# A two-layer hybrid decoder step: compressed attention rows as one block, sample rows of the scan at once, norms in pairs

## The chip, the cores and the metric

The kernel runs on one core of a Trainium2 chip. The metric is the device time of one execution in microseconds (us), the median over runs.

## The reference

One inference step of two layers over 512 prompt positions and 8 sample positions (one new token for each of 8 sequences with a past of 1024), model width 1024, all in float32. Layer 0 is a mixer, in which a Mamba-2 scan (32 heads in four groups) and sparse attention (16 heads in two key groups) share one input and one output projection. Layer 1 is a Conformer convolution with a layer norm inside. Behind each layer stands a feed-forward block with a width-3 convolution. Every one of the four parts is wrapped in two norms:

```python
def rms_norm(x, g):
    y = x * lax.rsqrt(jnp.mean(x * x, axis=-1, keepdims=True) + EPS)
    return y * g
...
hp = hp + rms_norm(mix, g[1])      # after the mixer or Conformer
...
hp = hp + rms_norm(f, g[3])        # after the feed-forward block
```

An attention output is the gated sum of three parts. The first is over compressed rows (31 for the prompt, each from 32 positions), the others over selected blocks and over a window of 512:

```python
s_c = jnp.einsum('btghd,bngd->btghn', qg, kc)
p_c = masked_softmax(s_c, m_c)
o_c = jnp.einsum('btghn,bngd->btghd', p_c, vc)
...
o = g[..., 0:1] * o_c + g[..., 1:2] * o_s + g[..., 2:3] * o_w
```

The scan's recurrence is `h = exp(dt a) h + dt B x`, `y = C h`, then `y + d_skip x`, times `silu(z)`. The prompt does it in four chunks of 128; a sample position takes a single step from its stored state.

## The kernel before, in words

**Layout.** Activations lie with channels on partitions: eight blocks of 128 channels (`KD`), 520 columns (512 prompt, 8 sample). Columns are worked in two halves, `HALF`, of 256 and 264. A float32 product is done as three products of a type with fewer bits (`split` makes a high part on ACT and a low part on DVE; `mm3` and `dense`, lines 312 to 314).

**Order of work.** A scheduler orders each engine's instructions by their dependences and the program's order; tiles are taken from pools with a number of buffers, and a pool's space is used again after release. Loads go mostly through SP's DMA queue, some through POOL's and ACT's.

**Attention** (`attention`, line 1102) runs 16 steps: four groups of four heads (`hg`) by four blocks of 128 queries (`b`). A step makes the scores of four heads with 32 compressed rows (`pc`) and with the window and selected rows (`Ps`), takes the softmax, and multiplies by the gates. `turned` (line 1182) transposes the weights of four heads into `pT` on PE, and splits them into `pth` (ACT) and `ptl` (DVE); two products with the values `VB` add up in `po`. The compressed part is the last of these turns, 32 rows by 512 columns, with `VC`. Tiles of the input projection for the scan (`xz_tile`) run between the steps; the last steps have none.

**Scan** (`scan_group`, line 1302) runs four groups `g` of four channel blocks `t`. Each loads `xs` and `cum` (the running decay of 512 positions, then 8 decays and 8 step sizes of the samples), makes decay products `dc`, states `hst` and `y`. The sample rows of a block are seven DVE operations at lines 1387 to 1395. POOL adds `yt` to `y` (line 1382) and splits the gated output of the group before (`x0ls`, `x1ls`), while PE does the output projection (`out_block`).

**Norms.** `postnorm` (line 377) takes a half of a part's result (`facc`), squares the eight blocks on ACT, adds squares on DVE in groups (`sumsq`, line 322), sums over partitions by a product with `ones`, takes Ln and Exp on ACT (`rstd`), and adds the normed blocks to `h` by two DVE operations each (lines 385 and 387). `prenorm` (line 358) gives the next part's input: scaled and split blocks of `h`, and the sum of their squares, whose root is put in later. `boundary` (line 520) chains them between two parts, named a to d. In ACT's code, functions stand in tables; `ACT_TABLE_LOAD` is the change of a table.

## Time and profile before

| what | value |
|---|---|
| median of 3 runs | 1960.81 us (1960.59 to 1962.98) |
| profiled execution, its own time | 1961.67 us |
| its span | 1959.9 us |
| PE busy | 1835.2 us, 94% |
| DVE busy | 1415.3 us, 72% |
| ACT busy | 974.4 us, 50% |
| POOL busy | 189.5 us, 10% |
| mean granted clock of PE | 0.97 |

The span is the time from the first to the last instruction that the profile shows. A busy PE is one with a product under way; products overlap, so that what a product costs is seen from its start to the next start. Idle time is shown with the work that ended it. Engines wait in the order of their own queues: a waiting instruction holds all behind it.

### The profile page before, as it was taken

To read this page: it belongs to the slowest core of one execution; us is meant where nothing else is said; L and a number is where in the kernel's file an instruction comes from. 1 tells how busy PE (TensorE), PEld (TensorE's weight loads), DVE (VectorE), ACT (ScalarE), POOL (GpSimd) and SP (SyncE) were. 2 spreads that over 40 slices of the span, in tenths; PEclk is the share of its full clock that TensorE was granted. 3 is DMA by queue.
4 is the path that set the end of the run, shared out by engine and by line. 5 is a ranking of instruction groups with operands and counts; after the bars stand their busy time and mean duration, and the time that the engine had idled before them with its cause. 6 is when DMAs were issued, how large, how long until landed. Compare 5 with 4: busy or idle time off the path is not lost.

```text
span 1959.9 us, 38005 instructions
## 1 busy us (share of the span) xinstructions
PE 1835.2 (94%) x14449; PEld 1706.1 (87%) x14449; DVE 1415.3 (72%) x3385; ACT 974.4 (50%) x2093; POOL 189.5 (10%) x226
## 2 busy tenths in 40 slices
PE   6998889999998799998999999999989899999997
PEld 5997888988887588987999999998667789999997
DVE  5764768888887698968667766574786865666766
ACT  3223446676666577646555433355127755444433
POOL 0000021101000003130000211001111000000000
PEclk9999998999998799989999999999999999999999
DMA  8446254444321274543245433222433223444421
GB/s 296 114 140 197 76 190 130 149 138 129 126 90 57 92 243 136 157 143 100 87 143 165 132 105 109 87 81 53 119 107 119 87 87 116 122 119 120 148 62 49
DMA packets 125947, 240.90 MB, mean 123 GB/s; under 512 B 16499, under 2 KB 63236, under 8 KB 125444
## 3 DMA queue, kind: packets, MB, share of 16 engines
q1 hardware_dynamic: 120676, 221.45, 36.9%
q0 software_dynamic: 4000, 13.73, 2.2%
q10 hardware_dynamic: 1088, 3.29, 0.5%
q8 instruction: 114, 1.87, 0.4%
q14 instruction: 69, 0.57, 0.1%
HBM read 200.75 MB, written 30.88 MB: 118 GB/s over the span
## 4 chain that ended last, share of the span: by engine, by line
PE 43%; DVE 5%; ACT 3%; DMA 2%; issue 1%; SPq 0%; POOL 0%; DVEq 0%; ACTq 0%; POOLq 0%
PE up L312 8%; PE up L313 8%; PE up L314 8%; PE dn L312 4%; PE dn L313 4%; PE dn L314 4%; PE dn L624 2%; PE pw L312 1%; PE pw L313 1%; PE pw L314 1%; PE ns L333 1%; DMA raw_dn<-in_w_down 1%; DVE xf L385 1%; DVE h L387 1%; DVE facc L631 1%
## 5 line engine op out<-in xcount | busy, mean ns | idle before, releaser
L312 PE MATMUL dn<-gh,wh_dn 128*128 128x256 f32 (+1 forms) x704 | 198.0, 285 | 4.8 <-ACT gh L463 2.6
L314 PE MATMUL dn<-gh,wl_dn 128*128 128x256 f32 (+1 forms) x704 | 198.9, 284 | 0.0
L313 PE MATMUL dn<-gl,wh_dn 128*128 128x256 f32 (+1 forms) x704 | 198.4, 283 | 0.0
L451 DVE SCALAR_TENSOR_TENSOR c<-up,vec,c 128x511 f32<-128x511 f32 (+2 forms) x216 | 138.9, 645 | 16.1 <-ACT c L448 15.7
L312 PEld LDWEIGHTS dn<-gh,wh_dn 128*128 128x128 f32 x704 | 131.5, 189 | 6.8 <-DVE facc L478 3.7
L313 PEld LDWEIGHTS dn<-gl,wh_dn 128*128 128x128 f32 x704 | 133.1, 189 | 0.1
L314 PEld LDWEIGHTS dn<-gh,wl_dn 128*128 128x128 f32 x704 | 132.8, 189 | 0.0
L464 POOL TENSOR_TENSOR gl<-gm,gh 128x520 fp32r<-128x520 f32 (+2 forms) x54 | 61.8, 1145 | 700.6 <-ACT gh L463 700.5
L446 DVE TENSOR_TENSOR up<-up,rsx 128x520 f32<-128x520 f32 (+2 forms) x108 | 65.0, 603 | 81.5 <-PE up L314 79.9
L478 DVE TENSOR_TENSOR facc<-dn,facc 128x256 f32<-128x256 f32 (+1 forms) x160 | 66.2, 423 | 66.4 <-PE dn L314 66.1
L293 ACT ACTIVATE wh_up<-raw_up 128x1024 fp32r<-128x1024 f32 x68 | 72.0, 1058 | 71.8 <-PE up L313 46.5
L312 PE MATMUL acc<-x0hm,wh_xz 128*128 128x256 f32 x320 | 96.3, 301 | 6.9 <-ACT u L1001 4.5
L294 DVE TENSOR_TENSOR wl_up<-raw_up,wh_up 128x1024 fp32r<-128x1024 f32 x68 | 83.1, 1222 | 23.0 <-ACT wh_up L293 22.9
L314 PE MATMUL acc<-x0hm,wl_xz 128*128 128x256 f32 x320 | 94.3, 295 | 0.0
L313 PE MATMUL acc<-x0lm,wh_xz 128*128 128x256 f32 x320 | 94.1, 294 | 0.0
L313 PE MATMUL acc<-x1lm,wh_xz 128*128 128x264 f32 x320 | 92.8, 290 | 0.0
L312 PE MATMUL acc<-x1hm,wh_xz 128*128 128x264 f32 x320 | 92.6, 289 | 0.0
L448 ACT ACTIVATE c<-up,vec 128x520 f32<-128x520 f32 (+2 forms) x108 | 74.9, 695 | 34.8 <-DVE up L446 34.4
L314 PE MATMUL acc<-x1hm,wl_xz 128*128 128x264 f32 x320 | 92.1, 288 | 0.0
L293 ACT ACTIVATE wh_dn<-raw_dn 128x1024 fp32r<-128x1024 f32 (+1 forms) x48 | 47.4, 988 | 87.7 <-PE dn L313 62.8
L294 DVE TENSOR_TENSOR ptl<-pT,pth 128x512 fp32r<-128x512 f32 (+1 forms) x96 | 65.0, 684 | 25.8 <-ACT pth L293 25.6
L293 ACT ACTIVATE pth<-pT 128x512 fp32r<-128x512 f32 (+1 forms) x96 | 56.3, 595 | 53.1 <-PE pT L1186 49.9
(584 smaller groups left out, 6859.7 us busy)
## 6 DMA issues: line engine op xcount, KB each, us to landing
raw_up<-in_w_up SPq DMA_DIRECT2D x68, 512.0 KB, 3.8
raw_xz<-in_w_in SPq DMA_DIRECT2D x40, 512.0 KB, 4.8
raw_dn<-in_w_down SPq DMA_DIRECT2D x32, 512.0 KB, 3.7
raw_wo<-in_w_out SPq DMA_DIRECT2D x24, 512.0 KB, 4.2
raw_pw<-in_w_pw SPq DMA_DIRECT2D x24, 512.0 KB, 3.8
spill<-uth SPq DMA_DIRECT2D x40, 260.0 KB, 2.0
st<-in_st SPq DMA_DIRECT2D x40, 256.0 KB, 4.2
cc<-in_c_cmp SPq DMA_DIRECT2D x64, 128.0 KB, 2.6
```

What stands on the lines that cost most here:

```text
L293: nc.scalar.activation(hi, src, AF.Copy)
L294: (eng or nc.vector).tensor_sub(lo, src, hi.bitcast(F32))
L312: nc.tensor.matmul(ps, hi[:, wc], xh, start=first, stop=False)
L313: nc.tensor.matmul(ps, hi[:, wc], xl, start=False, stop=False)
L314: nc.tensor.matmul(ps, lo[:, wc], xh, start=False, stop=last)
L333: nc.tensor.matmul(ps, ones, acc[:, :n], start=i < group, stop=i == len(ks) - 1)
L446: nc.vector.tensor_mul(u(a, e0), u(a, e0), rv[:, a:e0])
L448: nc.scalar.activation(c[:, rs], u(r0, r1), AF.Identity, bias=V("fb", l * 44 + mt), scale=W(2, mt))
L451: nc.vector.scalar_tensor_tensor(c[:, a:e], u(a - d, e - d), W(2 - d, mt), c[:, a:e], op0=ALU.mult, op1=ALU.add)
L464: nc.gpsimd.tensor_sub(gl[:, rs], gm[:, rs], gh[:, rs].bitcast(F32))
L478: nc.vector.tensor_add(f, ps, f)
L624: nc.tensor.matmul(ps[i * 32:i * 32 + 32], cw[m][:, 4 * q + i], x4[m][:, i, cs], start=q == 0, stop=q == NQ[m] - 1)
```

## The change

Three parts. **Compressed rows:** the weights of four heads over 32 compressed rows are transposed as one 128x128 block; `VC` holds, for each head, a block of 128 rows that is zero outside that head's 32 rows; eight products of 128x128 go into the four quarters of `po`, ahead of the other parts. The compressed values of a group are computed in four copies of rows (`vc`), and `VC` is split from them when the key group changes. The query rows are loaded a block at a time. **Sample rows:** two DMAs gather decays and step sizes of all 16 blocks into `cumS`; POOL copies the sample columns of `x` into `smp`; `sample_rows` does three operations for all blocks at the scan's start, `sample_group` four operations for each group. **Norms:** squares, sums of squares, the product with the norm and the addition to `h` are done for two blocks at once; the norm's gain is put in by ACT, in place, and the sums come in groups half as long, in pairs.

```diff
-SQE = 2
+SQE = 1
...
-SQP = 4
-SQR = 8
-SQL = (1, 4)
+SQP = 2
+SQR = 4
+SQL = (1, 2)
...
+    def sumsq2(ps, src, group):
+
+        n = ps.shape[-1]
+        for i in range(KD // 2):
+            sq = P["bq"].tile([128, 2, 266], F32, tag="sq", name="sq", bufs=3)[:, :, :n]
+            last = nc.scalar.activation(sq, src(2 * i), AF.Square)
+            if i % group:
+                nc.vector.tensor_add(acc, acc, sq)
+            else:
+                acc = sq
+            if i % group == group - 1 or i == KD // 2 - 1:
+                for j in range(2):
+                    nc.tensor.matmul(ps, ones, acc[:, j], start=i < group and j == 0, stop=i == KD // 2 - 1 and j == 1)
         return last
...
     def postnorm(wk, psp, hf, f, l, i, group=SQP, done=lambda k: None):
         c0, c1 = HALF[hf]
         ps = psp(c1 - c0)
-        last = sumsq(wk, ps, lambda k: f[:, k], range(KD), group)
+        last = sumsq2(ps, lambda k: f[:, k:k + 2], group)
+        for k in range(KD):
+            nc.scalar.activation(f[:, k], f[:, k], AF.Copy, scale=V("ng", (l * 4 + i) * 8 + k))
         r = rstd(wk, ps, 1.0 / D, "rs2", last if hf == 0 else None)
         done_["post%d" % hf] = done_["exp"]
-        for k in range(KD):
-            t = wk.tile([128, 266], F32, tag="xf", name="xf", bufs=XFB)
-            nc.vector.scalar_tensor_tensor(t[:, :c1 - c0], f[:, k], V("ng", (l * 4 + i) * 8 + k), r,
-                                           op0=ALU.mult, op1=ALU.mult)
-            nc.vector.tensor_add(h[:, k, c0:c1], h[:, k, c0:c1], t[:, :c1 - c0])
-            done(k)
+        for k in range(0, KD, 2):
+            f2, h2 = f[:, k:k + 2], h[:, k:k + 2, c0:c1]
+            nc.vector.tensor_mul(f2, f2, r[:, None].to_broadcast([128, 2, c1 - c0]))
+            nc.vector.tensor_add(h2, h2, f2)
+            done(k + 1)
...
+                VC = tp.tile([128, 4, 2, 64], F32R, tag="VC", name="VC", bufs=1)
+                nc.gpsimd.memset(VC.bitcast(F32), 0.0)
+                for hh in range(4):
+                    rw = slice(32 * hh, 32 * hh + 32)
+                    split(VC[rw, hh, 0], VC[rw, hh, 1], vc[rw, g])
             for b in range(4):
...
+                qh = tp.tile([128, 2, 128], F32, tag="qh", name="qh", bufs=2)
+                nc.sync.dma_start(qh, d_q[hg][:, :, b * 128:b * 128 + 128])
...
-                parts.append((VC[:, g], [pc[:, hh] for hh in range(4)], 32))
-                for k, (v, ps4, kn) in enumerate(parts):
-                    ph, pl = turned(ps4, kn)
...
+                pT = gen(128, "pT")
+                nc.tensor.transpose(pT, pc.rearrange("p h k -> p (h k)"), ident)
+                ph, pl = parted(pT)
+                for hh in range(4):
+                    for p in (ph, pl):
+                        nc.tensor.matmul(po[:, hh * 128:hh * 128 + 128], VC[:, hh].rearrange("p a d -> p (a d)"), p,
+                                         start=hh == 0 and p is ph, stop=False)
...
+        cd = tp.tile([128, 16, 2 * NB], F32, name="cumS")
+        for r in range(2):
+            nc.gpsimd.dma_start(cd[r * 64:r * 64 + 64], d_rows[r::2, S:528].rearrange("(o m) t -> o m t", o=1)
+                                .to_broadcast([64, 16, 2 * NB]))
+        xsk = tp.tile([128, 16, NB], F32, name="xskS")
+
+        def sample_rows():
+
+            nc.scalar.activation(smp[:, :, 1], cd[:, :, 0:NB], AF.Exp)
+            nc.vector.tensor_mul(xsk, smp[:, :, 0], VV("dsk")[:, :, None].to_broadcast([128, 16, NB]))
+            nc.vector.tensor_mul(smp[:, :, 0], smp[:, :, 0], cd[:, :, NB:])
+
+        def sample_group(g, y, bcs):
+
+            gs = slice(4 * g, 4 * g + 4)
+            ys = tp.tile([128, 4, NB], F32, tag="ys", name="ys", bufs=2)
+            nc.vector.tensor_mul(hC[:, gs], hC[:, gs], smp[:, gs, 1])
+            nc.vector.tensor_mul(ys, smp[:, gs, 0], bcs[:, 1][:, None, :].to_broadcast([128, 4, NB]))
+            nc.vector.tensor_add(hC[:, gs], hC[:, gs], xsk[:, gs])
+            nc.vector.tensor_add(y[:, :, S:T], hC[:, gs], ys)
...
-                dtx, es = smp[:, 4 * g + t, 0], E[:, S:T]
-                nc.vector.tensor_copy(smp[:, 4 * g + t, 1], es)
-                ys = tp.tile([128, 2, NB], F32, tag="ys", name="ys", bufs=2)
-                for r in range(2):
-                    sl = slice(r * 64, r * 64 + 64)
-                    nc.vector.tensor_mul(dtx[sl], xs[sl, S:T], cum[sl, r, T:528])
-                nc.vector.tensor_mul(ys[:, 0], hC[:, 4 * g + t], es)
-                nc.vector.tensor_mul(ys[:, 1], dtx, bcs[:, 1])
-                nc.vector.tensor_add(ys[:, 0], ys[:, 0], ys[:, 1])
-                nc.vector.scalar_tensor_tensor(y[:, t, S:T], xs[:, S:T], V("dsk", 4 * g + t), ys[:, 0],
-                                               op0=ALU.mult, op1=ALU.add)
+                if t == 0:
+                    sample_group(g, y, bcs)
```

Beside this, the squares and input copies of the mixer's first norm take their buffers from a pool of their own, `cum` and `E` lose their sample columns, and the stored states of the last group are read one group earlier.

The order of instructions moves at three places. First POOL at the end of the scan: `y<-y,yt` is the addition of line 1382, the others split the gated output for the output projection. Before:

```order
L294 TENSOR_TENSOR x0ls<-y,x0hs 128x256 x4
L294 TENSOR_TENSOR x1ls<-y,x1hs 128x264 x4
L1382 TENSOR_TENSOR y<-y,yt 128x384 x7
L294 TENSOR_TENSOR x0ls<-y,x0hs 128x256 x4
L294 TENSOR_TENSOR x1ls<-y,x1hs 128x264 x4
L1382 TENSOR_TENSOR y<-y,yt 128x384
L294 TENSOR_TENSOR x0ls<-y,x0hs 128x256 x4
L294 TENSOR_TENSOR x1ls<-y,x1hs 128x264 x4
```

After:

```order
L294 TENSOR_TENSOR x1ls<-y,x1hs 128x264 x4
L1442 TENSOR_TENSOR y<-y,yt 128x384 x8
L294 TENSOR_TENSOR x0ls<-y,x0hs 128x256 x4
L294 TENSOR_TENSOR x1ls<-y,x1hs 128x264 x4
L294 TENSOR_TENSOR x0ls<-y,x0hs 128x256 x4
L294 TENSOR_TENSOR x1ls<-y,x1hs 128x264 x4
```

The last addition stood behind eight splits of the group before, and now stands ahead of them.

Second DVE at the start of the scan, group 0, block 0 (`xde` is the input times step size and decay, `dc` the decay products, `hst` the states). Before:

```order
L1344 TENSOR_TENSOR xde<-xT,te 128x512
L1311 COPY bcs<-bcs 128x8
L1387 COPY smp<-E 128x8
L1392 TENSOR_TENSOR ys<-hC,E 128x8
L1393 TENSOR_TENSOR ys<-smp,bcs 128x8
L1394 TENSOR_TENSOR ys<-ys 128x8
L1395 SCALAR_TENSOR_TENSOR y<-xs,vec,ys 128x8
L1368 TENSOR_TENSOR dc<-dc,cbm 128x512
L1356 SCALAR_TENSOR_TENSOR hst<-hst,dec,states 128x64 x2
```

After:

```order
L1404 TENSOR_TENSOR xde<-xT,te 128x512
L1369 COPY bcs<-bcs 128x8
L1349 TENSOR_TENSOR smp<-smp,cumS 128x16x8
L1356 TENSOR_TENSOR ys<-smp,bcs 128x32
L1428 TENSOR_TENSOR dc<-dc,cbm 128x512
L1416 SCALAR_TENSOR_TENSOR hst<-hst,dec,states 128x64 x2
```

The operation that reads the gathered `cumS` stands ahead of the decay products and the states; ACT's exponential of `cumS` likewise stands ahead of `x0hn`, the split of attention's output.

Third ACT at boundary b, behind the first feed-forward block (`lnv` is the Ln and `rs` the Exp of a norm, `ge` the GELU of the feed-forward block, `wh_pw` the split of Conformer weights). Before:

```order
L459 ACTIVATE ge<-c_16270 128x264
L327 ACTIVATE sq<-facc 128x256
L339 ACT_TABLE_LOAD
L293 ACTIVATE wh_pw_16615<-raw_pw_16613 128x1024
L448 ACTIVATE c_16302<-up,vec 128x264
L348 ACTIVATE lnv<-ns,epsT 128x256
L349 ACTIVATE rs_16101<-lnv 128x256
```

After:

```order
L341 ACTIVATE sq<-facc 128x2x256
L354 ACT_TABLE_LOAD
L471 ACTIVATE fstg<-up 128x10
L476 ACT_TABLE_LOAD
L476 ACTIVATE ge<-c_16195 128x264
L398 ACTIVATE facc<-facc,vec 128x256 x2
L293 ACTIVATE wh_pw_16516<-raw_pw_16514 128x1024
L465 ACTIVATE c_16227<-up,vec 128x264
L363 ACT_TABLE_LOAD
L363 ACTIVATE lnv<-ns,epsT 128x256
L364 ACT_TABLE_LOAD
L364 ACTIVATE rs_16053<-lnv 128x256
```

The load for the norm now stands ahead of the last GELU, so that a load back follows at once, and Ln and Exp have one each. In the whole program there are 33 table loads, where there were 27.

## Rows read from the trace of the kernel before

**Rows 1.** The page, first part: busy time of each engine, share, instructions.
```profile
PE 1835.2 (94%) x14449; PEld 1706.1 (87%) x14449; DVE 1415.3 (72%) x3385; ACT 974.4 (50%) x2093; POOL 189.5 (10%) x226
```

**Rows 2.** Busy by stretch (PE, PEld, DVE, ACT, POOL), clock, DMA share, GB/s.
```profile
300.00:606.00 306.00, 297.06 (x2309) 268.63 (x2307) 260.61 (x823) 199.78 (x500) 26.35 (x39) 0.98 0.40 123
606.00:668.00 62.00, 51.30 (x219) 34.59 (x216) 44.95 (x129) 34.31 (x84) 0.00 (x0) 0.78 0.07 22
690.00:850.00 160.00, 153.81 (x1300) 143.46 (x1297) 147.99 (x432) 111.12 (x280) 35.38 (x37) 0.99 0.54 166
910.00:960.00 50.00, 39.72 (x278) 36.95 (x278) 38.97 (x88) 33.02 (x66) 5.80 (x7) 0.90 0.15 46
```

**Rows 3.** Timeline of PE, 606 to 625 us: start, length, engine, line, operation.
```profile
607.10 0.28 PE L1124 MATMUL sc<-KL,QS 128*128 128x256 f32 x1
607.22 0.28 PE L1123 MATMUL sc<-KH,QS 128*128 128x256 f32 x1
...
607.83 0.39 PE L1199 MATMUL po<-pth,VB 128*128 128x512 f32 x1
608.05 0.60 PE L1186 MATMUL pT<-cst,pt 128*128 128x128 f32 x4
```

**Rows 4.** Timeline of PE, 338 to 342 us, inside attention.
```profile
339.29 0.49 PE L1199 MATMUL po<-pth,VC 32*128 32x512 f32 x1
339.71 0.38 PE L312 MATMUL acc<-x0hm,wh_xz 128*128 128x256 f32 x1
```

**Rows 5.** Timeline of all engines, 663.5 to 668.5 us, last attention step.
```profile
664.41 0.59 ACT L293 ACTIVATE pth<-pT 32x512 fp32r<-32x512 f32 x1 [0.73 <-DVE ptl L294]
...
665.03 0.68 DVE L294 TENSOR_TENSOR ptl<-pT,pth 32x512 fp32r<-32x512 f32 x1 [0.62 <-ACT pth L293]
```

**Rows 6.** Timeline, 668 to 690 us, start of the scan; idle time in brackets.
```profile
670.84 0.16 DVE L1387 COPY smp<-E 128x8 f32<-128x8 f32 x1
...
670.91 0.16 DVE L1392 TENSOR_TENSOR ys<-hC,E 128x8 f32<-128x8 f32 x1
...
681.20 0.34 DVE L1391 TENSOR_TENSOR smp<-xs,cum 64x8 f32<-64x8 f32 x2 [2.61 <-DMA cum<-d_rows]
```

**Rows 7.** Timeline, 846 to 854 us, end of the scan.
```profile
847.93 0.75 DVE L1378 SCALAR_TENSOR_TENSOR y<-xs,vec,yd 128x512 f32<-128x512 f32 x1 [0.59 <-PE yd L1372]
...
850.95 0.99 POOL L1382 TENSOR_TENSOR y<-y,yt 128x384 f32<-128x384 f32 x1
...
851.96 0.70 DVE L1397 TENSOR_TENSOR y<-y,zt 128x520 f32<-128x520 f32 x1 [2.92 <-POOL y L1382]
```

**Rows 8.** Groups by line and form, whole span: DVE, ACT and PE.
```profile
L651 DVE TENSOR_TENSOR facc<-facc,nmu 128x528 f32<-128x528 f32 x4 | 2.6, 704 | 2.5 <-ACT nmu L649 2.5
...
L366 ACT ACTIVATE x0ha<-h,vec 128x256 fp32r<-128x256 f32 x8 | 4.0, 498 | 0.4 <-DVE h L387 0.4
...
L333 PE MATMUL ns<-sq,ones 128*128 128x264 f32 x56 | 17.2, 414 | 5.9 <-DVE sq L329 5.9
```

**Rows 9.** Timeline of ACT, 905 to 950 us: a table load.
```profile
939.92 1.28 ACT L459 ACT_TABLE_LOAD   x1
941.21 0.42 ACT L459 ACTIVATE ge<-c 128x256 f32<-128x256 f32 x1
```

**Rows 10.** Timeline, 1947 to 1957 us, the last norm.
```profile
1947.88 0.42 ACT L327 ACTIVATE sq<-facc 128x264 f32<-128x264 f32 x1 [0.76 <-DVE facc L478]
...
1949.58 0.48 ACT L348 ACTIVATE lnv<-ns,epsT 128x264 f32<-128x264 f32 x1 [1.27 <-PE ns L333]
...
1950.54 0.90 DVE L385 SCALAR_TENSOR_TENSOR xf<-facc,vec,rs 128x264 f32<-128x264 f32 x2 [1.77 <-ACT rs L349]
...
1952.05 0.89 DVE L385 SCALAR_TENSOR_TENSOR xf<-facc,vec,rs 128x264 f32<-128x264 f32 x2
```

**Rows 11.** DMA issues on the POOL queue: count, size, median us to landing.
```profile
st<-in_st POOLq DMA_DIRECT2D x24, 256.0 KB, 3.6
...
cum<-d_rows POOLq DMA_DIRECT2D x1, 528.0 KB, 8.3
```

More of the change, by code (lines that the diff above doesn't have):

```diff
@@ L370, in prenorm @@
         ps = psp(c1 - c0 - o)
-        last = sumsq(wk, ps, lambda k: src(k)[:, o:], range(KD), group)
+        last = sumsq2(ps, lambda k: src(k)[:, :, o:], group)
         rstd(wk, ps, 1.0 / D, "rs1", last if hf else None, rs[:, c0 + o:c1])
     def hrows(hf):
-        return lambda k: h[:, k, X0[hf]:HALF[hf][1]]
+        return lambda k: h[:, k:min(k + 2, KD), X0[hf]:HALF[hf][1]]
     def postnorm(wk, psp, hf, f, l, i, group=SQP, done=lambda k: None):
@@ L652, in norm @@
                 ps = ns(n)
-                last = sumsq(bk, ps, lambda k: c[:, k], range(KD), SQL[hf])
+                last = sumsq2(ps, lambda k: c[:, k:k + 2], SQL[hf])
                 r = rstd(bk, ps, 1.0 / D, "rsl", last)
@@ L1180, in attention, with parted @@
                             nc.vector.tensor_scalar(p, p, mx[:, 2, hh, r:r + 1], None, op0=ALU.mult)
-                def turned(ps4, kn):
-                    pT = gen(512, "pT")
-                    for hh in range(4):
-                        nc.tensor.transpose(pT[0:kn, hh * 128:hh * 128 + 128], ps4[hh], ident)
-                    ph, pl = (tp.tile([128, 512], F32R, tag="pt" + p, name="pt" + p, bufs=THB)[0:kn] for p in "hl")
-                    split(ph, pl, pT[0:kn])
+                def parted(pT):
+                    ph, pl = (tp.tile([128, 512], F32R, tag="pt" + p, name="pt" + p, bufs=THB)[:, :pT.shape[-1]]
+                              for p in "hl")
+                    split(ph, pl, pT)
@@ new lines, in attention @@
+                nc.tensor.transpose(pT, pc.rearrange("p h k -> p (h k)"), ident)
[4 more added lines that the diff above has]
+                                         start=hh == 0 and p is ph, stop=False)
+                for n in range(b + 1):
+                    for r in range(2):
+                        pT = gen(512, "pT")
+                        for hh in range(4):
+                            nc.tensor.transpose(pT[:, hh * 128:hh * 128 + 128], Ps[hh][:, r, n * 128:n * 128 + 128], ident)
+                        ph, pl = parted(pT)
+                        v = VB[:, 1 - r, n, g].rearrange("p a d -> p (a d)")
+                        nc.tensor.matmul(po, v, ph, start=False, stop=False)
+                        last = nc.tensor.matmul(po, v, pl, start=False, stop=n == b and r == 1)
@@ L1228, in row_loads @@
             q.dma_start(xs, spill[g * 10 + t])
-            cum = pool.tile([128, 2, 528], F32, tag="cum", name="cum", bufs=1 if g == t == 0 else XSB)
+            cum = pool.tile([128, 2, S], F32, tag="cum", name="cum", bufs=1 if g == t == 0 else XSB)
             k = g * 8 + 2 * t
-            q.dma_start(cum, d_rows[k:k + 2, :].rearrange("(o h) t -> o h t", o=1).to_broadcast([128, 2, 528]))
+            q.dma_start(cum, d_rows[k:k + 2, 0:S].rearrange("(o h) t -> o h t", o=1).to_broadcast([128, 2, S]))
             return xs, cum
@@ L1323, in scan_group @@
             y = tp.tile([128, 4, T], F32, tag="y", name="y", bufs=YB)
-            if g >= HG:
-                later = state_rows(tp, g)
+            if g == HG - 1:
+                later = state_rows(tp, HG)
+            if g == 0:
+                sample_rows()
             for t in range(4):
@@ L1664, in begin @@
         return after
-    with tc.tile_pool(name="wum", bufs=3, side="right") as P["wu"]:
+    with tc.tile_pool(name="wum", bufs=3, side="right") as P["wu"], tc.tile_pool(name="bm", bufs=1, side="right") as P["bm"]:
         new = mixer(begin)()
```

53 lines of the change are left out of this document (27 added, 26 removed).

## The prediction

> **What bounds the kernel now.** I read the page first, then the busy times by stretch, then the timeline where a stretch loses time. PE is busy for 94% of the span and DVE for 72% [rows 1], so work taken off DVE is worth something only where PE waits for it. By stretch [rows 2]: from 300 to 606 us, where attention runs with the input projection between its products, PE is busy 297 of 306 us at clock 0.98 and DVE 261, so PE's own work decides. From 606 to 668 us the projection is used up; PE is busy 51 of 62 us, the granted clock is 0.78, and each product waits for the ACT and DVE steps ahead of it. From 690 to 850 us (scan and output projection) PE has 154 and DVE 148 of 160 us: two engines nearly full, each waiting for the other now and then. At the first norm boundary, 910 to 960 us, PE has 40 and DVE 39 of 50: there PE waits for chains of short DVE and ACT operations. The sum is made against the profiled execution, 1961.7 us (span 1959.9 and 1.8 around it), which is 0.9 above the median of the runs.
>
> **Compressed rows, steps inside 300 to 606 us.** A step now gives the compressed part four 32-row transposes and two 32x512 products. Each product holds PE 0.42 us, from its start to the next start [rows 4], while a 128x512 one holds it 0.22 (607.83 to 608.05) and a 256-wide one 0.12 [rows 3]. Around each of the two stands some 0.1 us more, and four transposes at 0.11 are 0.44: 1.48 us in a step. After, it is one transpose and eight 128x128 products. No 128-wide product of that type stands in the trace: below I bound it by the 256-wide 0.12 (a narrower one should not take longer), above by 0.22, since [rows 4] show that a product of unusual shape can run at half the rate. I take 0.12, the row that is nearer in width: 0.11 + 8 x 0.12 = 1.07 us, 0.41 less a step, 12 steps: **-5 us** (ends: -5 and, at 0.22, 12 x 0.39 = +5). DVE and ACT lose about 0.4 and 0.3 us a step, which PE covers. The query rows come in 16 loads of a quarter block each instead of four, two buffers deep, a whole step (about 20 us) ahead: nothing.
>
> **The attention's tail, 606 to 668 us.** Here the turn itself is on the path: ACT 0.59, DVE 0.68 us for 32x512, then the products, and in the last step nothing else is left for PE [rows 5]. The new turn is 128x128, stands first in its step, and ends before the softmax of the four heads is through; after the last window part no turn is left. Four steps, 0.6 to 1.2 us each less the narrow products' time that PE now spends: **-3 us** (ends -5 and +2, the latter with products of 0.22).
>
> **Scan, sample rows.** Removed are seven DVE operations in each of 16 blocks. Alone each is 0.16 to 0.23 us, but starts follow 0.07 us apart where nothing is waited for [rows 6]; a block is between 0.5 and 1.2 us, I take 0.75: 12 us in all. Added are four operations a group and two more once, about 0.2 us each: 3.6. Net 8.4 us of DVE, 2 of them before 690 us, where DVE waits for loads anyhow [rows 6]. In 690 to 850 us DVE is 92% and PE 96% busy, so at most 6.4, and I take two thirds: **-4 us** (ends 0 and -6.4). The 16 copies on POOL fall in 300 to 606 us, where POOL has 26 us of work: nothing.
>
> What is added there is a **wait**: DVE's product with the gathered rows stands behind `xde` and ahead of the decay products and the state recurrence, and ACT's exponential stands ahead of the split of the attention's output, which PE needs for its first output products. Both wait for two DMAs issued by POOL only once the attention's buffers are released, near 668 us. Issue and landing lie between 3.6 us (the POOL queue's loads of whole rows) and 8.3 us (the first `cum`) [rows 11]; these two have some thousand pieces of 64 bytes each, more than either. DVE would need them at 670.8 us. Today DVE idles 2.6 us until 681.2 for the next block's `cum` [rows 6], which takes up a delay of some 3 to 5 us. Landing at 672 costs nothing, at 685 about 8 us. I take **+1** (ends 0 and +8).
>
> **POOL at the scan's end.** The last `y<-y,yt` starts at 850.95 behind eight splits of the group before, while DVE sat idle 2.9 us for it [rows 7]; the order after puts all eight additions ahead of the splits. DVE's next operation and the whole gated norm behind it move by about 2.2 us, as the input was ready near 848.7: **-2 us** (ends 0 and -2.9).
>
> **Norms in pairs.** For one half, the product with the norm and the addition to `h` take 1.5 us a pair of blocks now (1950.54 to 1952.05) and would take two operations of 0.62 to 0.70 us [rows 8, 10]: 0.25 us less, 1 us a half. Sums of squares in pairs save DVE another 0.6 to 0.8 us a norm. ACT gains 0.1 us a pair of squares and pays eight scaled copies, of the kind of the 0.5 us `x0ha`, 0.41 us apart: 3.3 us a half [rows 8]. Most stand behind the square of their own pair, so that only two are left when the last square is done, 0.8 us, and PE's sum plus DVE's addition took 1.28 us there (1948.30 to 1949.58) [rows 10]. There are 23 more products with `ones`, each two instructions of 0.41 us [rows 8] that overlap by half, 0.4 us: 9 us of PE, over half of it in PE's waits, so +3 to +5. Six table loads more at 1.28 us [rows 9]: at the second boundary Ln and Exp each get their own, and the second lies between them, on the path of three norms: +3. The end loses 1 us, the first and third boundaries, where DVE's queue holds PE, perhaps 2 and 1. Together -1 -2 -1 +3 +3 = **+2 us** (ends -8 and +12).
>
> First the row, then a rule that speaks against the change: after a table load of 1.283 us `ge` starts 0.01 us after it ends [rows 9]. The Trainium skill ("ScalarE: Activation LUTs", What ACT_TABLE_LOAD costs) gives each switch 1.38 us of drain on top, 2.66 in all. No drain is seen here, so the sum stays; by the rule the six loads would cost 16 us of ACT instead of 8, and the sum would be about 4 us higher.
>
> The terms: -5 -3 -4 +1 -2 +2 = -11, so 1950.7 for a profiled execution and **1950 us** for the median.
>
> **Rivals.**
> 1. *The narrow products run at 0.22 us.* For: the 32-row form's 0.42 shows that shape matters, and PE has no room in 300 to 606 us. Against: 256-wide runs at 0.12. It adds 0.8 x 16 = 13 us to the forecast: 1963.
> 2. *ACT takes DVE's place on the norm chains* (slower). If the scheduler's order lets all eight copies stand ahead of Ln, each of eight halves waits 3.3 - 1.3 = 2 us longer, 16 in all, and the six loads add 7.7, with the attention and scan gains of 13 kept: 1961.7 - 13 + 16 + 7.7 - 0.9 = 1971. It decides from the point where more than three copies (1.28 / 0.41) stand between last square and Ln. The order shows two in most halves and four at the first boundary's first half, which speaks against.
> 3. *PE hides the scan's savings*: PE is 96% busy there and the moved POOL work only fills another wait. Without -4 and -2: 1956.
> 4. *The gathered rows land late*, stalling DVE and ACT at once at the scan's start: +7 on the forecast, 1957. Against: the POOL queue's loads issued beside a DVE that was 85% busy landed in 3.6 us [rows 11]. The Trainium skill ("SBUF — State Buffer", A bandwidth-pool intuition that's wrong) says that a DMA issued by GpSimd can wait for its descriptors while a DVE operation holds their shared port, 3.1 us in place of 0.6; by it the two would come some 5 us later. The 24 loads from that queue do not show it.
> 5. *The chains give back more*: 6.4 and 2.9 us in the scan, 5 in the tail, the norms' lower end of -8: 1936.
>
> **How the numbers follow.** Forecast 0.44, rivals in order 0.20, 0.10, 0.10, 0.06, 0.10. A measurement of this kernel can tell about 0.2%, 4 us, so faster means under 1956.9 and slower over 1964.7. Faster: 0.40 of the forecast, 0.03 of rival 1, 0.06 of rival 3, 0.03 of rival 4, 0.10 of rival 5: 0.62. Slower: 0.07 of rival 1 and 0.09 of rival 2: 0.16. The rest, 0.22, is no change. The range 1937 to 1965 leaves out rival 2, the upper part of rival 1 and the lower half of rival 5, together less than 0.2; the forecast's own range is 1941 to 1957.
>
> **What would show it.** In the profile after: products of `po` with VC 0.12 us apart (right) or 0.22 (rival 1); 300 to 606 us about 5 shorter; no wait above 1 us of DVE or ACT for `cumS` (rival 4 otherwise); the last `y<-y,yt` right behind `yt`; Ln of each half behind PE's sum, not behind a copy of `facc` (rival 2). The prediction is wrong if the attention stretch is not shorter, or if the boundaries lengthen by more than 5 us together.

## The result, and the profile of the changed kernel

The changed kernel takes 1977.6 us (median of 4 runs, 1974.2 to 1981.4) where the kernel before, run beside it, took 1960.7: ratio 1.0089, 95% interval 1.0069 to 1.0108. It is **slower by 0.9%**; the forecast was 1950 with a range of 1937 to 1965. The profiled execution spans 1977.4 us against 1959.9.

The page of the changed kernel, first part, the columns as in [rows 1]:

```profile
PE 1839.6 (93%) x14543; PEld 1722.0 (87%) x14543; DVE 1385.6 (70%) x3183; ACT 995.8 (50%) x2107; POOL 196.1 (10%) x246
```

PE is busy 4 us more, DVE 30 less, ACT 21 more, and the span is 17.5 longer: PE waits longer. Where, shows a division of both traces into stretches. I take the starts of named PE products as their bounds, because these exist in every form of the kernel: the first `acc<-x0hm,wh_xz` (input projection), the first `BT<-cst,Bm` (scan), the last `acc<-x1hs,wh_wo` (output projection), the first `up<-x0ha,wh_up` (behind the first norm boundary), the first `up<-x0ha,wh_ue` (last group of the first feed-forward), the first `pw<-x1hb,wh_pw` (behind the second boundary), and the same for the second feed-forward.

| us | to projection | attention, tail | scan | boundary 1 | feed-forward 1 | boundary 2 | conformer, boundary 3 | feed-forward 2 | end | span |
|---|---|---|---|---|---|---|---|---|---|---|
| before | 192.4 | 473.8 | 240.8 | 55.2 | 299.3 | 88.9 | 248.7 | 298.2 | 62.5 | 1959.9 |
| changed | 190.0 | 467.7 | 241.4 | 53.0 | 299.9 | **102.8** | 250.3 | 299.5 | **72.8** | 1977.4 |

The mixer and boundary 1 together give back 10 us; 2.4 of them lie ahead of the projection, in a stretch that takes between 189.8 and 194.5 us in all the forms below, and tell nothing. Two places cost 24: the second boundary (13.9) and the end (10.3). Both are the last group of a feed-forward with the norm behind it.

**The attention came out as forecast, the scan only in part.** PE is busy 6 us less between 300 and 606 us than in [rows 2] (the same columns):

```profile
300.00:606.00 306.00, 291.22 (x2318) 269.02 (x2318) 260.60 (x841) 197.37 (x506) 25.07 (x52) 0.99 0.40 123
```

The narrow products stand 0.11 us apart (timeline of PE inside attention), where a 32x512 one held PE 0.42 [rows 4]:

```profile
343.64 0.28 PE L1226 MATMUL po<-pth,VC 128*128 128x128 f32 x1
343.75 0.27 PE L1226 MATMUL po<-ptl,VC 128*128 128x128 f32 x1
```

The gathered rows are issued at 660.12, and DVE waits for them 1.90 us at the scan's start (timeline, all engines). The first decay products come 7.2 us behind the scan's start instead of 6.5; by the fourth, 21.9 against 21.7, the difference is nearly gone. At the scan's end the wait of 2.92 us for POOL [rows 7] is gone; 0.27 us for another load is left:

```profile
660.12 1.67 POOL L1341 DMA_DIRECT2D cumS<-d_rows  x2 [87.19 <-PE cb L1379]
...
664.47 0.29 DVE L1349 TENSOR_TENSOR smp<-smp,cumS 128x128 f32<-128x128 f32 x1 [1.90 <-DMA cumS<-d_rows]
```

```profile
833.17 1.01 POOL L1442 TENSOR_TENSOR y<-y,yt 128x384 f32<-128x384 f32 x1 [4.45 <-DVE y L1438]
834.22 0.70 DVE L1447 TENSOR_TENSOR y<-y,zt 128x520 f32<-128x520 f32 x1 [0.27 <-DMA st<-in_st]
```

This last addition starts 175.5 us behind the scan's start where it was 184.8. The scan's stretch is no shorter for it (241.4 against 240.8), because PE now has more of the output projection still ahead of it there. From the last addition to the stretch's end, first the kernel before, then the changed one (columns as in [rows 2]):

```profile
850.95:907.00 56.05, 51.98 (x376) 48.69 (x376) 39.06 (x69) 29.25 (x53) 7.45 (x10) 0.91 0.49 161
833.17:899.00 65.83, 60.76 (x461) 58.51 (x460) 48.84 (x74) 39.76 (x74) 14.94 (x17) 0.97 0.43 139
```

**The second boundary.** First the kernel before: timeline around the first half's norm (start, length, engine, line, operation, idle time before and its releaser).

```profile
1297.23 0.41 ACT L327 ACTIVATE sq<-facc 128x256 f32<-128x256 f32 x1
...
1297.66 1.28 ACT L339 ACT_TABLE_LOAD   x1
...
1301.60 0.47 ACT L348 ACTIVATE lnv<-ns,epsT 128x256 f32<-128x256 f32 x1 [1.10 <-PE ns L333]
...
1302.11 0.42 ACT L349 ACTIVATE rs<-lnv 128x256 f32<-128x256 f32 x1
...
1302.56 0.88 DVE L385 SCALAR_TENSOR_TENSOR xf<-facc,vec,rs 128x256 f32<-128x256 f32 x2 [0.34 <-ACT rs L349]
1303.35 0.43 DVE L461 TENSOR_TENSOR gm<-ge,c 128x264 f32<-128x264 f32 x1
...
1304.29 0.81 PE L312 MATMUL dn<-gh,wh_dn 128*128 128x264 f32 x2 [2.60 <-ACT gh L463]
```

From the end of the last square (1297.64) to the end of `rs` (1302.53) are 4.9 us with one table load, and what ends PE's wait is the last `gh` of the other half, whose `gm` stands on DVE behind two `xf` products. PE then has the 78 remaining `dn` products of the second half to mix with the `pw` products that need the norm. Now the changed kernel, same view and place:

```profile
1288.34 0.64 ACT L341 ACTIVATE sq<-facc 128x512 f32<-128x512 f32 x1 [1.35 <-DVE facc L495]
...
1288.99 1.28 ACT L354 ACT_TABLE_LOAD   x1
...
1290.47 1.28 ACT L476 ACT_TABLE_LOAD   x1
...
1291.77 0.43 ACT L476 ACTIVATE ge<-c 128x264 f32<-128x264 f32 x1
...
1292.10 0.89 ACT L398 ACTIVATE facc<-facc,vec 128x256 f32<-128x256 f32 x2
...
1294.41 1.28 ACT L363 ACT_TABLE_LOAD   x1
...
1295.71 0.47 ACT L363 ACTIVATE lnv<-ns,epsT 128x256 f32<-128x256 f32 x1
1296.20 1.28 ACT L364 ACT_TABLE_LOAD   x1
1297.49 0.42 ACT L364 ACTIVATE rs<-lnv 128x256 f32<-128x256 f32 x1
1297.94 2.50 DVE L403 TENSOR_TENSOR facc<-facc,rs 128x512 f32<-128x512 f32 x4 [2.28 <-ACT rs L364]
1300.36 0.48 DVE L468 SCALAR_TENSOR_TENSOR c<-up,vec,c 128x256 f32<-128x256 f32 x1
1300.75 2.49 DVE L404 TENSOR_TENSOR h<-h,facc 128x512 f32<-128x512 f32 x4
...
1302.03 0.80 PE L312 MATMUL pw<-x0hb,wh_pw 128*128 128x256 f32 x2 [8.89 <-ACT x0hb L381]
1303.15 0.43 DVE L478 TENSOR_TENSOR gm<-ge,c 128x264 f32<-128x264 f32 x1
...
1309.60 0.41 PE L312 MATMUL dn<-gh,wh_dn 128*128 128x264 f32 x2
```

From the last square's end (1288.98) to the end of `rs` (1297.91) are now 8.9 us: a GELU (`ge`) stands between the load for Ln and Ln itself, so four loads of 1.28 us lie in it instead of one. All four coarse products stand ahead of the convolution's last step (`c`), and `gm` is behind the additions as well, so the other half's `gh` is late too. And PE's own row is another: 32 `pw` products, which need the norm, stand ahead of the 78 `dn` products of the second half that were to fill the wait. PE idles 8.9 us, and runs at half clock after it (granted clock 0.50 in the window from 1300 us on):

```profile
1300.00:1305.00 5.00, 1.77 (x6) 1.47 (x7) 5.00 (x11) 3.71 (x10) 0.59 (x1) 0.50 0.12 45
```

The second half's norm has two loads more as well, at 1327.21 ahead of Ln and at 1329.01 ahead of Exp, where the kernel before has none. The work behind it on ACT is late by that much, and PE waits 5.11 us instead of 2.81. First the kernel before, then the changed one:

```profile
1328.61 0.58 PE L312 MATMUL pw<-x0hb,wh_pw 128*128 128x256 f32 x1 [2.81 <-ACT glu L586]
1332.56 0.58 PE L312 MATMUL pw<-x0hb,wh_pw 128*128 128x256 f32 x1 [5.11 <-ACT glu L603]
```

**The end.** Timeline of the changed kernel at the last feed-forward's end:

```profile
1941.80 0.29 PE L314 MATMUL up<-x1hc,wl_ue 128*128 128x266 f32 x1
...
1946.61 3.05 DVE L403 TENSOR_TENSOR facc<-facc,rs 128x512 f32<-128x512 f32 x4
...
1947.06 0.51 PE L312 MATMUL dn<-gh,wh_dn 128*128 128x264 f32 x2 [1.92 <-ACT gh L480]
...
1949.59 1.88 DVE L404 TENSOR_TENSOR h<-h,facc 128x512 f32<-128x512 f32 x3
1951.39 0.42 DVE L495 TENSOR_TENSOR facc<-dn,facc 128x264 f32<-128x264 f32 x1
...
1951.86 0.59 PE L312 MATMUL dn<-gh,wh_dn 128*128 128x264 f32 x1 [3.15 <-DVE facc L495]
```

The very last `up` product of the second half now stands behind 24 `dn` products of the first half; in the kernel before it stood ahead of them. Its chain (`up`, `c`, `gm`, `gh`) therefore ends late, and PE, which by then has filled both PSUM buffers of `dn` with all that needs no last `gh`, waits 1.92 us. Then it waits 3.15 us more: the addition that frees a `dn` buffer (`facc`, L495) stands on DVE behind four products and three additions of the norm. The granted clock behind these waits (a window of 5 us, columns as in [rows 2]) is 0.50, the 1.2 GHz level:

```profile
1950.00:1955.00 5.00, 3.14 (x14) 3.14 (x15) 2.84 (x7) 1.56 (x3) 0.00 (x0) 0.50 0.25 88
```

The last norm itself is shorter, as forecast: its products and additions take 5.0 us (1968.28 to 1973.3) where those of [rows 10], a pair each 1.5 us, took 6.1 (1950.54 to 1956.6).

```profile
1968.28 2.56 DVE L403 TENSOR_TENSOR facc<-facc,rs 128x528 f32<-128x528 f32 x4 [2.89 <-ACT rs L364]
1970.76 2.56 DVE L404 TENSOR_TENSOR h<-h,facc 128x528 f32<-128x528 f32 x4
```

### The profile page after: what moved, and what is told of

Same layout as the page of the kernel before. It is cut to its first block, busy times and chain, and to the rows that moved or that the text cites. A ratio compares the mean times of both kernels' runs of the same rounds, so it can differ in the third digit from the quotient of the medians.

```text
span 1977.4 us, 38051 instructions
## 1 busy us (share of the span) xinstructions
PE 1839.6 (93%) x14543; PEld 1722.0 (87%) x14543; DVE 1385.6 (70%) x3183; ACT 995.8 (50%) x2107; POOL 196.1 (10%) x246
## 4 chain that ended last, share of the span: by engine, by line
PE 68%; DVE 12%; ACT 7%; DMA 6%; issue 4%; SPq 2%; POOL 0%; DVEq 0%; ACTq 0%; POOLq 0%
PE up L312 8%; PE up L313 8%; PE up L314 8%; PE dn L312 5%; PE acc L312 5%; PE dn L313 4%; PE dn L314 4%; PE acc L313 4%; PE acc L314 4%; PE cmpAB L953 2%; DMA st<-in_st 2%; PE dn L641 2%; PE pw L312 1%; PE pw L313 1%; PE pw L314 1%
## 5 line engine op out<-in xcount | busy, mean ns | idle before, releaser
L463 DVE TENSOR_TENSOR up<-up,rsx 128x520 f32<-128x520 f32 (+2 forms) x108 | 65.2, 604 | 90.9 <-PE up L314 89.3
L495 DVE TENSOR_TENSOR facc<-dn,facc 128x256 f32<-128x256 f32 (+1 forms) x160 | 66.5, 424 | 86.4 <-PE dn L314 86.0
L293 ACT ACTIVATE wh_up<-raw_up 128x1024 fp32r<-128x1024 f32 x68 | 72.2, 1062 | 77.7 <-PE up L313 52.4
L294 DVE TENSOR_TENSOR wl_dn<-raw_dn,wh_dn 128x1024 fp32r<-128x1024 f32 (+1 forms) x48 | 54.9, 1143 | 36.0 <-ACT wh_dn L293 35.6
L1198 ACT ACTIVATE pt<-sc,mx 128x128 f32<-128x128 f32 (+3 forms) x128 | 66.5, 528 | 23.5 <-DVE mx L1157 17.8
```

The lines of the kernel that those rows point to most:

```text
L293: nc.scalar.activation(hi, src, AF.Copy)
L294: (eng or nc.vector).tensor_sub(lo, src, hi.bitcast(F32))
L463: nc.vector.tensor_mul(u(a, e0), u(a, e0), rv[:, a:e0])
L495: nc.vector.tensor_add(f, ps, f)
L1198: nc.scalar.activation(pt[:, r, 0:nw], sv[r], AF.Exp, bias=mx[:, 0, hh, r:r + 1], scale=-1.0, accum_out=mx[:, 1, hh, r:r + 1])
```

## The experiments

Ratios are to the kernel before, run beside each form. At the end of this section one table has the stretches of all.

**1. Is it the norms?** The norms undone in the changed kernel (`sumsq`, `prenorm`, `postnorm`, the groups and the pools as before), and the norms put alone into the kernel before.

> The changed kernel with its norms written as in the kernel before (sums of squares, products and additions block by block, no copies of facc), the compressed rows and the sample rows kept. Theory A (the norms in pairs cost about 27 us, the other two parts gained about 10 to 15, as the alignment of the two traces says): 1945 to 1953, and the stretch from the second norm boundary to the end no longer than in the kernel before. Rival B (the loss at the norms comes from the other parts, which moved PE's work of the mixer so that the boundaries lie otherwise): 1965 or more, with the second boundary still about 10 us longer than before.

> The kernel before with the norms in pairs alone (attention and scan untouched). Theory A: 1960.8 + 27 = 1988, at least 1980, with the second boundary and the end both about 10 us longer. Rival B: near 1961 to 1967. If this and the run with the norms as before do not add up (the sum of the two differences against +17), the parts act on one another.

Measured 0.9967 (0.9955 to 0.9978), 1953.0 us, and 1.0165 (1.0148 to 1.0182), 1988.9 us. Theory A holds: everything lost is lost by the norms, 1.2% or 24 us in the changed kernel and 32 alone. The two do not add up: -6 and +32 against the +17 of the changed kernel, so the parts act on one another.

**2. Which part of the norms?** Squares in pairs kept, but product and addition block by block with the gain on DVE, no copies of `facc`:

```diff
-        for k in range(KD):
-            nc.scalar.activation(f[:, k], f[:, k], AF.Copy, scale=V("ng", (l * 4 + i) * 8 + k))
...
-            nc.vector.tensor_mul(f2, f2, r[:, None].to_broadcast([128, 2, c1 - c0]))
-            nc.vector.tensor_add(h2, h2, f2)
...
+            nc.vector.scalar_tensor_tensor(t[:, :c1 - c0], f[:, k], V("ng", (l * 4 + i) * 8 + k), r,
+                                           op0=ALU.mult, op1=ALU.mult)
+            nc.vector.tensor_add(h[:, k, c0:c1], h[:, k, c0:c1], t[:, :c1 - c0])
```

and, apart from it, the pair product written into a buffer of its own instead of over `facc`:

```diff
-            nc.vector.tensor_mul(f2, f2, r[:, None].to_broadcast([128, 2, c1 - c0]))
-            nc.vector.tensor_add(h2, h2, f2)
+            t = P["bq"].tile([128, 2, 266], F32, tag="sq", name="xf", bufs=3)[:, :, :c1 - c0]
+            nc.vector.tensor_mul(t, f2, r[:, None].to_broadcast([128, 2, c1 - c0]))
+            nc.vector.tensor_add(h2, h2, t)
```

> The changed kernel with squares in pairs kept, but product and addition block by block with the gain on DVE, and no copies of facc on ACT. Theory A1 (the loss comes from the coarse products and additions and the copies: the order puts all multiplies ahead of the first addition, the first input of the next stage is late, and PE's other products stand behind it): 1950 to 1958. Rival A2 (the table loads: this form issues 35 of them against 33 and 27 before): 1977 or more. Rival A3 (the squares in pairs, with 23 more products with ones): 1970 or more.

> The changed kernel with the pair product written into a buffer of its own (three of them) in place of over facc, so that at most three products stand ahead of the first addition; copies and table loads stay (35 loads). If the number of multiplies ahead of the first addition is what counts, 0.6 us less on each of four halves: about 1974. If the order on PE (the other half's products put behind the ones that wait for the norm) is what counts: no change against the changed kernel, 1977.

Measured 1.0084 (1.0068 to 1.0101) and 1.0092 (1.0075 to 1.0109). My theory A1 fell: without a copy on ACT and without a coarse product the kernel is as slow as with them, and the buffer that limits the row of products changes nothing. Between the loads (A2) and the squares (A3) the 1974.6 us of the first form, 2 under what A2 asked for, do not decide; the reordered forms of experiments 4 and 6, which keep the squares in pairs, later put A3 aside. Its ACT timeline at the second boundary has the loads all the same:

```profile
1290.96 1.28 ACT L354 ACT_TABLE_LOAD   x1
...
1292.45 1.28 ACT L475 ACT_TABLE_LOAD   x1
...
1295.60 1.28 ACT L363 ACT_TABLE_LOAD   x1
...
1297.38 1.28 ACT L364 ACT_TABLE_LOAD   x1
```

and its PE row at the end is that of the changed kernel product for product: 24 `dn` of the first half, one `up`, 18 `dn` of the second, the four sums of squares, 30 `dn`. At the second boundary it is not: there `dn` and `pw` products are mixed as in the kernel before, PE waits for the last `gh`, and the stretch loses 10.0 us all the same (98.9 against 88.9). `rs` ends 8.2 us behind the last square:

```profile
1301.26 0.81 PE L312 MATMUL dn<-gh,wh_dn 128*128 128x264 f32 x2 [6.22 <-ACT gh L479]
...
1301.86 0.63 PE L312 MATMUL pw<-x0hb,wh_pw 128*128 128x256 f32 x2
```

So the slow forms share the loads at the second boundary and PE's row at the end; at the second boundary the changed kernel has both. These two I then changed one at a time.

**3. The loads alone.** The preload behind the last scaled copy instead of behind the last square:

```diff
-            nc.scalar.activation(f[:, k], f[:, k], AF.Copy, scale=V("ng", (l * 4 + i) * 8 + k))
+            last = nc.scalar.activation(f[:, k], f[:, k], AF.Copy, scale=V("ng", (l * 4 + i) * 8 + k))
```

> The changed kernel with the preload of the table for Ln and Exp placed behind the last scaled copy of facc instead of behind the last square: 26 table loads instead of 33, and no GELU between the preload and Ln. PE's order stays that of the changed kernel. Theory L (table loads on the chain from the last square to the norm are most of the loss): 1962 to 1967. Theory O (PE's order is most of it: the other half's down products come too late to fill the norm's wait): 1971 to 1975, 3 to 5 less than the changed kernel from the second boundary alone, the end as before.

Measured 1.0055 (1.0040 to 1.0071), 1971.0 us: as theory O said. At the second boundary one load is left and `rs` ends 5.1 us behind the last square instead of 8.9, but PE still waits for the norm with the `pw` products at the head of its row (timeline, all engines):

```profile
1289.28 1.28 ACT L354 ACT_TABLE_LOAD   x1
...
1292.79 0.42 ACT L364 ACTIVATE rs<-lnv 128x256 f32<-128x256 f32 x1
...
1297.36 0.79 PE L312 MATMUL pw<-x0hb,wh_pw 128*128 128x256 f32 x2 [5.11 <-ACT x0hb L381]
```

The stretch goes from 102.8 to 96.7 us. The end, where the load was never followed by a GELU, goes from 72.8 to 70.8.

**4. PE's row.** In the last group, both halves' `up` products and GELUs are written ahead of the first half's `dn` products:

```diff
                     for hf in range(2):
                         for m in range(*skew):
                             g[m] = pair(m, (hf,), wu[m - skew[0]], g.get(m))
+                    for hf in range(2):
                         gs = [g[m] for m in range(m0, m1)]
                         for m in range(KD):
```

> The changed kernel with one thing written in another order: in the last group of each feed-forward, the up products and GELUs of both halves are written ahead of the down products of the first half. In the order that results, the 24 last up products are no longer split by down products, the second half's 16 down products stand whole ahead of the sum of squares, and there are 26 table loads. Theory O: the end loses some 10 of its extra time and the second boundary some 8: 1957 to 1963. Theory D (DVE's coarse products and additions hold the chain whatever PE does): 1970 or more.

> Control: the norms as before, with the up products written first in the same way. If PE's order was already good there, this gains nothing: 1951 to 1956 (the form without the reordering gave 0.9967 of before). Theory O says that the distance of the paired norms to this one is then small, 4 to 8 us, instead of 24; theory D says that it stays at 20 or more.

Measured 0.9972 (0.9959 to 0.9986), 1953.8 us, and 0.9978 (0.9966 to 0.9989). The first is better than the 1957 to 1963 I had expected: that one edit takes back 1.17%, 23 of the 24 us that were lost, and the paired norms are then no slower than the old ones. It moves more than PE's row: the last `up` products come earlier, and with them their chain on ACT and DVE. In the timeline at the end, `rs` and the four products are where the sum wanted them, and PE passes through without a wait (the row of PE right behind the sums of squares is a `dn` product of the second half):

```profile
1926.92 1.02 PE L348 MATMUL ns<-sq,ones 128*128 128x256 f32 x4
...
1927.59 0.47 PE L312 MATMUL dn<-gh,wh_dn 128*128 128x264 f32 x1
...
1929.30 0.40 ACT L364 ACTIVATE rs<-lnv 128x256 f32<-128x256 f32 x1
...
1929.79 2.49 DVE L403 TENSOR_TENSOR facc<-facc,rs 128x512 f32<-128x512 f32 x4
```

This edit also brought the loads to 26, so the two places were told apart by making it in one feed-forward only:

> The changed kernel with the up products written first in the first feed-forward only: PE's row differs from the changed kernel's only at the second norm boundary, and there are 26 table loads; the end is as in the changed kernel. If each place has its own loss and the order decides it: the 15 us that the boundary lost against the fully reordered form come back, 1961 to 1964 (ratio 1.001), and the end still adds 8 to 10. If the places act on one another, more than 1968.

> The changed kernel with the up products written first in the second feed-forward only: PE's row differs only in the last 30 us, with the 33 table loads of the changed kernel. Expected: the end gives back 8 to 10, the second boundary still loses its 13: 1968 to 1971 (ratio 1.005).

Measured 1.0013 (0.9998 to 1.0028) and 1.0058 (1.0040 to 1.0077): the second boundary gives back 0.76%, 15 us, and the end 0.31%, 6 us. They add up to 1.07 of the 1.17% that both together gave back.

**5. The reverse.** Norms as before, and the second half's last three `up` products held behind the first half's last `dn` product, which gives PE the changed kernel's row at the end, but for two more late `up` products:

```diff
...
+            with tc.issue_after(hold.ins) if hold is not None and k == KD - 1 else ExitStack():
+                mm3(ps, w, slice(k * 128, k * 128 + 128), xh[:, k, cs], xl[:, k, cs], k == 0, k == KD - 1)
...
+                            g[m] = pair(m, (hf,), wu[m - skew[0]], g.get(m), mm if hf and m == skew[1] - 1 else None)
```

> The reverse of the reordering: norms as before, with the compressed rows and the sample rows, and the last three up products of the second half held behind the first half's last down product in both feed-forwards. Near the end PE's row then reads as in the changed kernel (12 down products of the second half, the sum of squares, 20 more), with 28 table loads and the fine pieces of the kernel before. Theory O (the order on PE alone costs it): 6 to 14 more than the 1953 of the form with the norms as before: 1959 to 1967. If the coarse pieces on DVE are needed for the loss: 1951 to 1956.

Measured 0.9993 (0.9982 to 1.0005), 0.26% or 5 us over the form without the hold. That is less than the 6 to 14 that theory O asked for and more than its rival did, because only the end came out as meant: 69.0 us there against 62.7, while at the second boundary PE's row stayed as it was (89.5 and 89.5). The wait is the one of the changed kernel, for the late `gh`:

```profile
1926.88 0.42 ACT L464 ACTIVATE gh<-gm 128x264 fp32r<-128x264 f32 x1 [1.21 <-DVE gm L462]
...
1927.35 0.81 PE L312 MATMUL dn<-gh,wh_dn 128*128 128x264 f32 x2 [2.72 <-ACT gh L464]
```

So fine pieces in the bad order lose 6.3 us at the end. The changed kernel's coarse ones lost 10.3; the second wait, of 3.15 us for the buffer, is 0.45 here.

**6. Controls.** The reordering in the kernel before, and with squares in pairs but products by block:

> The kernel before with nothing changed but the up products of the last group written first. Its order on PE was already one in which the second half's down products fill the norm's wait, so 1956 to 1963, no difference that can be told; a gain of more than 4 would mean that the reordering is an improvement of its own and not a repair.

> The changed kernel with the up products written first, squares in pairs, and product and addition block by block with the gain on DVE (no copies of facc); 28 table loads. Here the order puts 48 down products of the second half in one row and all their sums of squares at the end. By my sum the pair products are worth 1 a half at the end and nothing elsewhere: 1953 to 1957, within the measurement of the form with pair products (0.9972). A time of 1948 or less would make it the best version; one of 1965 or more would mean that the order of the sums at the end matters too.

Measured 1.0030 (1.0020 to 1.0041) and 1.0003 (0.9992 to 1.0015). In the kernel before the reordering loses 0.3%, where I had expected no difference: its second boundary takes 92.5 instead of 88.9. So it is no improvement of its own; which row is good depends on the pieces around it. The other form misses my expectation by 3 to 7 us; it takes 93.1 at the same place, and its different row at the end costs nothing (64.2).

**7. The other two parts, each alone.**

> The kernel before with the compressed rows as one block alone (sample rows and norms as before). By the forecast's terms: 5 + 3 = 8 us less, 1953. By the aligned traces of the form with the norms as before, where the attention ends 5 us earlier: 1954 to 1956; then the sample rows gave about 1 to 2 of the 6.5.

> The kernel before with the scan's sample rows for all blocks at once alone. By the forecast's terms -4 + 1 - 2: 1955. The form with compressed rows as well measured 0.9967 and the compressed rows alone 1.0016, so if the two add up, this one is at 0.995, 1951.

Measured 1.0016 (1.0001 to 1.0031) and 0.9988 (0.9978 to 0.9998): no gain and 2 us, where I expected 5 to 8 and 6 to 10. The stretches show a part of why; the profiled execution of the first was 5 us shorter than its median and that of the second 5 us longer. Each saves what it should in its place (attention 461.5 instead of 473.8; scan 237.1 instead of 240.8), and each loses 5 to 7 us at the first boundary (60.0 and 61.8 instead of 55.2), whose code neither touches. In both, PE's row is cut elsewhere: two products of a sum of squares stand behind 43 and 38 of a block of 48 `up` products, not behind all 48 as in the kernel before. With compressed rows alone PE waits there 4.96 us for a step of the convolution (`c`) where it waited 3.93, and 2.13 where it had no such wait. What moves a row there was not tried.

The stretches in us, from the profile of each form (single profiled executions; forms that share a piece of code differ there by some 1 us in the feed-forwards, by 3 in the scan, by up to 6 in attention with compressed rows and by up to 7 in the stretch of the third boundary; the stretch to the projection, 189.8 to 194.5, is left out):

| form | attention, tail | scan | boundary 1 | feed-forward 1 | boundary 2 | conformer, boundary 3 | feed-forward 2 | end | ratio |
|---|---|---|---|---|---|---|---|---|---|
| before | 473.8 | 240.8 | 55.2 | 299.3 | 88.9 | 248.7 | 298.2 | 62.5 | 1 |
| changed | 467.7 | 241.4 | 53.0 | 299.9 | 102.8 | 250.3 | 299.5 | 72.8 | 1.0089 |
| norms as before | 467.6 | 236.7 | 54.3 | 298.1 | 89.5 | 254.4 | 297.3 | 62.7 | 0.9967 |
| norms alone | 473.4 | 241.9 | 51.7 | 300.0 | 104.0 | 250.2 | 299.5 | 72.8 | 1.0165 |
| products by block | 466.8 | 238.7 | 55.0 | 300.4 | 98.9 | 249.9 | 299.5 | 71.4 | 1.0084 |
| pair product in own buffer | 464.6 | 240.4 | 52.4 | 299.6 | 101.2 | 250.9 | 299.5 | 71.8 | 1.0092 |
| load behind copies | 465.0 | 242.1 | 51.8 | 300.4 | 96.7 | 250.5 | 299.5 | 70.8 | 1.0055 |
| ups first | 465.3 | 238.8 | 51.7 | 299.8 | 87.4 | 250.5 | 299.5 | 64.6 | 0.9972 |
| ups first, products by block | 466.0 | 238.7 | 54.3 | 300.1 | 93.1 | 251.2 | 299.5 | 64.2 | 1.0003 |
| in feed-forward 1 only | 464.1 | 239.6 | 51.9 | 300.3 | 87.4 | 250.6 | 299.5 | 72.7 | 1.0013 |
| in feed-forward 2 only | 465.0 | 240.2 | 51.7 | 299.6 | 103.6 | 249.5 | 299.5 | 64.6 | 1.0058 |
| late ups, norms as before | 463.5 | 237.6 | 54.3 | 298.0 | 89.5 | 253.6 | 297.3 | 69.0 | 0.9993 |
| ups first, norms as before | 467.4 | 238.5 | 54.6 | 297.4 | 92.7 | 250.8 | 297.3 | 62.6 | 0.9978 |
| before, ups first | 472.3 | 240.4 | 55.4 | 298.2 | 92.5 | 248.4 | 298.2 | 62.4 | 1.0030 |
| compressed rows alone | 461.5 | 242.4 | 60.0 | 298.0 | 89.0 | 251.3 | 297.3 | 62.7 | 1.0016 |
| sample rows alone | 473.3 | 237.1 | 61.8 | 298.4 | 89.3 | 247.1 | 297.3 | 62.4 | 0.9988 |

Three forms beat both kernels by 0.2% and more: the changed kernel with the norms as before (0.9967), with the `up` products first (0.9972) and with both (0.9978). Their intervals overlap, and which is best stays open.

## Why the prediction was wrong, step by step

- **Compressed rows, -5 and -3: right in their stretch.** The stretch to the scan's start is 472.3 to 473.8 us in the three forms shown without them beside the kernel before, and 461.5 to 467.7 in the twelve with them: 5 to 12 less. The products run at 0.11 us, below the lower bound, and rival 1 (0.22) is out. That the whole kernel gains by it is not shown: alone, they measure 1.0016.
- **Sample rows -4, the wait +1, POOL's order -2: the sum of -5 was nearly right where the norms are as before** (236.7 to 238.5 with them, 240.4 to 242.4 without: -4). The gathered rows cost a wait of 1.9 us, over the 1 us that was to be rival 4's sign, but 0.7 us at the scan's start and not rival 4's 7. POOL's wait at the end went. With squares in pairs 238.7 to 242.1 are measured against 241.9 without the sample rows, so there only 0 to 3 of it arrives. That is rival 3 in part: the last addition comes 9 us earlier in the scan, and PE gives most of it back behind it, with 461 products to do instead of 376.
- **Norms in pairs, +2: this step failed.** It was 24 us in place of 2. The working took the lengths of the pieces and the number of loads from the rows, and held the rest of the order as it was. The pieces were priced rightly: the last norm lost its 1 us, and with the order repaired the paired norms measure within 0.1% of the old ones, as +2 says. The six loads were there, priced at +3; undoing them brought back 0.34%, 7 us, because at the second boundary a GELU had come between the preload and Ln and three more loads with it, all on one chain. The largest item, a move of PE's own row, was not in the sum at all: at the last group of both feed-forwards PE's products stand in another order. At the second boundary 32 products that need the norm stand ahead of the 78 `dn` products that were to fill its wait; at the end one `up` product behind 24 `dn` products makes the last `gh` late, and the additions that free PE's buffers stand behind the coarse products on DVE. Putting the ups first alone gives back 15 and 6 us at these places.
- **The sum of rival 5** is off by 1 to 2 us: its own terms give 1934.5, not 1936. Nothing hangs on it.
- **Rival 2** named the right side (slower) and a wrong mechanism. Its copies are two behind the last square, as I had read, and the form without any copy is as slow. Its loads were part of it.
- **What I had said would show it wrong** did: the boundaries lengthened by more than 5 us together. What I had not said is that the order of PE at the two last groups could be compared before the run: I had looked at the order of the engines that run the edited lines, and not at that of the engine that waits for them.
- **A second, smaller error:** gains in the mixer were carried unchanged to the end. With the norms as before the trace is 11.5 us ahead at the first feed-forward (950.7 against 962.2), and 6.5 arrive; 5.7 are lost in the stretch of the third boundary, 254.4 against 248.7, whose code is the same in both. Why was not tried.

Of the 24 us, then, in the order in which they were undone: loads about 7, PE's row with the coarse pieces behind it about 17. At the second boundary the split depends on that order: the loads with the old mixed row lose 10.0 us (products by block), the new row without the loads 7.8 (load behind copies), both together 13.9. Open is why paired norms lengthen the steady part of the feed-forwards by 1 to 2 us, and by how much PE's row and DVE's queue share the loss at the second boundary.

## What to carry to other kernels

Where a scheduler sets the order, coarser instructions are a change of order first and of work second: before pricing a piece, compare the row of the busiest engine at every place where another chain was to fill its wait. Look there for three things: whether work that needs the result now stands ahead of work that does not, whether the additions that free its buffers stand behind a long row on another engine, and whether a function of another table has come between a preload and its use. And when such a change measures badly, repair the order before throwing the change away: one moved loop gave back 23 of 24 us here.

## What the runs showed of the hardware

- 128x128 products follow each other at 0.11 us, 256-wide ones at 0.12 and 512-wide ones at 0.22 [rows 3]: below 256 columns a product is hardly cheaper, and eight narrow ones (8 x 0.11 = 0.9) replace two of 32x512 at 0.42 [rows 4] about evenly.
- The Trainium skill ("ScalarE: Activation LUTs", What ACT_TABLE_LOAD costs) adds 1.38 us of drain to a load. No drain shows here either: the load at 1297.38 of the form with products by block starts right behind an Ln that ended at 1297.36, and Exp starts at 1298.68, as its 1.28 us end.
- After 8.9 us without a product at the second boundary PE's granted clock was 0.50. The following 32 products took 7.6 us (1302.03 to 1309.60) where 32 at 0.12 would take 3.8; 1.2 us of that is a wait for `x0lb`, and the rest comes from starts 0.21 us apart up to 1308.25, and 0.12 after it. So this wait of PE cost some 2 us more behind it.
